# One transformer layer on one core: the last 256 tokens of the last down-product with tokens on partitions

## The chip, the cores and the metric

The kernel runs on one core of one Trainium2 chip. The metric is the device time of one execution in microseconds (us). The kernel before takes 1895.25 us, the median of three runs (1892.29 to 1896.35).

## The reference

One layer works on 1024 tokens of 1024 features, with 16 learned meta tokens ahead of them that are dropped at the end. All arithmetic is float32.

```
h = h + 0.5 * rmsnorm(swiglu(rmsnorm(h, g0), w_in[0], w_out[0]), g1)
h = h + rmsnorm(mlstm_mixer(rmsnorm(h, g2)), g3)
h = h + 0.5 * rmsnorm(swiglu(rmsnorm(h, g4), w_in[1], w_out[1]), g5)
return h[:, 16:]

swiglu(x)  = (silu(x @ w_in[:, :2816]) * (x @ w_in[:, 2816:])) @ w_out    # w_out: 2816 x 1024
rmsnorm(x) = x * rsqrt(mean(x * x) + 1e-6) * g                            # mean over the 1024 features
```

The change is in the last product by `w_out` (the "down product"), and in the norm, the addition of the residual h and the output that follow it.

## The kernel before

Features lie on the 128 partitions and tokens run along the free axis. A block of 512 tokens of the 1024 features is then 8 tiles of 128 x 512. A float32 product is done as three passes of matmuls in the format fp32r: each operand is split into a high and a low part, and high x high, high x low and low x high are summed in PSUM (`PASSES`). The split of a weight tile (`split_w`, lines 136 to 141) is a copy to fp32r on ScalarE (L139) and a subtraction on VectorE (L140).

Weights come by the DMA queue of SyncE (SPq) in the sequence of a list, `order`, into four raw buffers, are split in two halves into seven buffers, and are taken by `next_w`, which keeps loads and splits some tiles ahead. The 22 inner features (each 128 of the 2816) are cut into three segments, `SEGS`: 14 to 21, 0 to 7, and 8 to 13. The activations of one segment come back from DRAM by `load_a`, which splits them too (L327 on VectorE).

`down` does one segment for one block of tokens: for each of the 8 output tiles it takes a weight tile, runs the matmuls of its 6 or 8 inner features into a PSUM bank `pd` (L574, stationary = 128 x 128 of the weights, moving = the activations), and puts the sum into the result block `r`: ScalarE copies it for the first segment (L586), VectorE adds it for the others (L588). So each block has three sums per output tile.

The last down product has two blocks: C, the first 512 tokens, and E, the last 512. `downs` does C's three segments, then E's first two. The third segment of E is done twice, with its weights fetched a second time (names with `2x`): for E0 (E's first 256 tokens), then for E1 (the other 256). The norm of a block is a generator, `last_norm`: `rstd` squares the 8 result tiles (ScalarE), adds them on VectorE (L282), sums over partitions by a matmul with ones (`cb_ms`, L291), takes the root in 13 small steps on VectorE (L296 to L304), and brings the factors to all partitions by a matmul (`cb_rb`, L313) and a copy. Then two wide operations per tile follow, times gain and factor (L399) and plus residual (L400), and an output DMA. `tasks` and `tick` lay the steps of such generators between the matmuls of the product that runs beside them: C's norm lies in E's first segment, E0's norm in E1's third. E1's norm comes after all products, in a variant that divides the work among three engines (`fast`).

The program is written in this sequence; a scheduler of the framework then sets the sequence on each engine, and each engine works through its own in order.

Of the kernel before, what the change touches and what calls it, by code (L numbers as in the profile page):

```python
# [20 lines left out]
F32 = mybir.dt.float32  # L21
# [32 lines left out]
@with_exitstack  # L54
def trunk(ctx: ExitStack, tc: tile.TileContext, xa, xb, w1, w2, wqk, wv, wog, wo, par, cst, out):
    nc = tc.nc
# [326 lines left out]

    def last_norm(b, gi, scale, res, name, fast, queue=None):

        rs, n, e = R[b.i], b.n, b.s0 + b.n
        ret = []
        yield from rstd(lambda k: rs[:, k, b.s0 : e], n, scale, name, ret, fast)
        r = ret[0]
        for k in range(KT):  # L390
            y = rs[:, k, b.s0 : e]
            if fast:
                act.activation(y, y, AF.Copy, scale=gains[:, gi, k : k + 1])
        for k in (0, 1, 2, 3, 4, 7, 5, 6) if fast else range(KT):
            y = rs[:, k, b.s0 : e]
            if fast:
                (pool if k == 7 else vec).tensor_tensor(y, y, r[:, :n], ALU.mult)
            else:
                vec.scalar_tensor_tensor(y, y, gains[:, gi, k : k + 1], r[:, :n], ALU.mult, ALU.mult)  # L399
            (pool if fast and k in (0, 2, 7) else vec).tensor_tensor(y, y, res(k), ALU.add)  # L400
            if not fast:
                queue.dma_start(out[b.i, :, k, b.s0 : e], y)
            elif k in (1, 3, 5, 6):
                j = k - k % 2
                (act if k % 4 == 1 else sp).dma_start(
                    out[b.i, :, j : j + 2, b.s0 : e], rs[:, j : j + 2, b.s0 : e])
            yield

# [183 lines left out]

    def downs(li, b0, b1, Z, a0, second):
# [87 lines left out]
    tasks.append(split_x(A, 2, xh[0][0], range(4), "ca0"))  # L681
    c2 = next(phase)
    xh[0][1] = operand(Z[4], "xh0_1")
# [386 lines left out]
    es.close()  # L1070
    es_al, alp[0] = stage("al3", 4)

    def resid(k):
# [7 lines left out]
    res = block(Z[1], "res")  # L1081
    for k in range(0, KT, 2):
        pool.dma_start(res[:, k : k + 2, :512], h2[1][:, k : k + 2])
    c2 = next(phase)
    finish()
    E0, E1 = E.part(0, 256), E.part(256, 256)
    ends = [last_norm(q, 5, 0.5, lambda k, q=q: res[:, k, q.s0 : q.s0 + 256], f"cb1{q.s0}", q is E1, sp)
            for q in (E0, E1)]
# [4 lines left out]
    for _ in ends[1]:  # L1093
        pass
    es_al.close()


def _layout(inputs):
# [4 lines left out]
    def tiles(w):  # L1103
# [19 lines left out]
    return {  # L1123
        "xa": xt[:, :, :528], "xb": xt[:, :, 528:], "w1": w1, "w2": w2, "wqk": tiles(wa[:, 0:1024]), "wv": wv,
        "wog": tiles(wa[:, 2048:3072]), "wo": tiles(f["a_w_out"][0]), "par": par, "cst": cst,
# [16 lines left out]
```

## Time and profile before

| | us |
|---|---|
| median of the three runs | 1895.25 |
| profiled execution | 1892.53 |
| its span | 1890.4 |
| TensorE busy in it | 1854.1 (98%) |
| VectorE busy in it | 1283.0 (68%) |
| ScalarE busy in it | 750.2 (40%) |

The span runs from the first to the last instruction of one profiled execution; its own time is a little longer. The mean granted clock of TensorE was 0.994 of full speed. PE stands for matmuls on TensorE, PEld for its weight loads, DVE for VectorE, ACT for ScalarE, POOL for GpSimd, SP for SyncE. L574 is line 574 of the kernel before. A time such as 1620.24 is measured from the start of the span.

### The profile page before, as it was taken

How to read it: one execution, taken by the hardware profiler on the slowest of the kernel's cores; microseconds unless marked ns; L12 is line 12 of the kernel's file. 1: busy time of each engine (PE TensorE's matmuls, PEld its weight loads, DVE VectorE, ACT ScalarE, POOL GpSimd, SP SyncE). 2: the span in 40 equal slices, each digit the busy share in tenths (PEclk: the TensorE clock that was granted, in tenths of full speed). 3: DMA queues.
4: the chain of work that ended last, by engine and by line, in shares of the span. 5: the costliest groups of instructions: out<-in, count | busy, mean ns of one | idle time of the engine just before them, and what ended most of it. 6: DMA issues, size and time to landing. Idle time of an engine off the chain costs nothing.

```text
span 1890.4 us, 34012 instructions
## 1 busy us (share of the span) xinstructions
PE 1854.1 (98%) x13428; PEld 1733.9 (92%) x13428; DVE 1283.0 (68%) x2302; ACT 750.2 (40%) x1324; POOL 204.9 (11%) x367
## 2 busy tenths in 40 slices
PE   7999999999999999999999999999999999999995
PEld 7999999999999888999798878999999999888885
DVE  6857888887356746863774568686877777456547
ACT  5433332233334423544544445563332222344323
POOL 1210000000000002201002112221000000000100
PEclk9999999999999999999999999999999999999998
DMA  8655454445346424634435546765454444555633
GB/s 310 203 199 174 164 175 147 137 146 190 116 156 185 150 81 147 193 96 140 132 100 171 174 169 212 248 227 200 163 169 165 152 146 156 159 162 159 206 112 95
DMA packets 112270, 311.28 MB, mean 165 GB/s; under 512 B 14208, under 2 KB 24896, under 8 KB 112112
## 3 DMA queue, kind: packets, MB, share of 16 engines
q1 hardware_dynamic: 83280, 215.49, 36.5%
q0 software_dynamic: 28288, 93.10, 13.7%
q8 instruction: 106, 1.74, 0.4%
q10 hardware_dynamic: 544, 0.52, 0.1%
q14 instruction: 52, 0.43, 0.1%
HBM read 239.18 MB, written 69.88 MB: 163 GB/s over the span
## 4 chain that ended last, share of the span: by engine, by line
PE 92%; issue 3%; DMA 2%; DVE 2%; ACT 1%; POOL 0%; SPq 0%; DVEq 0%; POOLq 0%; ACTq 0%
PE pd L574 26%; PE py L417 13%; PE pw L417 13%; PE pz L417 7%; PE hy L417 6%; PE hx L417 6%; PE po L1003 5%; PE wog_ps L727 5%; PE wqk_ps L727 4%; PE pv L838 4%; PE pn L950 1%; DMA xa<-xa 1%; DMA o<-xa 1%; PE pn L944 0%; DMA W<-nmd 0%
## 5 line engine op out<-in xcount | busy, mean ns | idle before, releaser
L574 PE MATMUL pd<-a,w 128*128 128x512 f32 (+2 forms) x2640 | 481.1, 344 | 0.0
L574 PEld LDWEIGHTS pd<-a,w 128*128 128x128 f32 x2640 | 415.4, 188 | 62.9
L417 PE MATMUL py<-x,w1j_p 128*128 128x264 f32 (+1 forms) x2112 | 266.7, 282 | 0.0
L417 PE MATMUL pw<-x,w1j_p 128*128 128x264 f32 (+1 forms) x2112 | 266.7, 282 | 0.0
L417 PEld LDWEIGHTS pw<-x,w1j_p 128*128 128x128 f32 x2112 | 258.4, 188 | 0.0
L417 PEld LDWEIGHTS py<-x,w1j_p 128*128 128x128 f32 x2112 | 258.3, 188 | 0.0
L139 ACT CAST w1j_p<-w1j_s 128x512 fp32r<-128x512 f32 x176 | 109.3, 621 | 314.7 <-PE py L417 184.9
L140 DVE TENSOR_TENSOR w<-w_raw,w 128x512 fp32r<-128x512 f32 x192 | 123.4, 646 | 152.4 <-ACT w L139 152.1
L139 ACT CAST w<-w_raw 128x512 fp32r<-128x512 f32 x192 | 112.2, 585 | 209.6 <-PE pd L574 192.4
L417 PE MATMUL hx<-x,w1a 128*128 128x264 f32 (+1 forms) x1056 | 137.4, 286 | 10.4 <-ACT w1a L139 8.2
L417 PEld LDWEIGHTS hx<-x,w1a 128*128 128x128 f32 x1056 | 131.9, 191 | 11.1 <-ACT w1a L139 8.2
L417 PE MATMUL hy<-x,w1a 128*128 128x264 f32 (+1 forms) x1056 | 135.5, 283 | 2.7 <-DVE hc L446 2.4
L417 PE MATMUL pz<-x,w1j_p 128*128 128x264 f32 (+1 forms) x1056 | 133.4, 282 | 0.0
L417 PEld LDWEIGHTS hy<-x,w1a 128*128 128x128 f32 x1056 | 130.0, 189 | 3.5 <-DVE hc L446 2.8
L140 DVE TENSOR_TENSOR w1j_p<-w1j_s,w1j_p 128x512 fp32r<-128x512 f32 x176 | 121.8, 692 | 11.6 <-ACT w1j_p L139 9.9
L417 PEld LDWEIGHTS pz<-x,w1j_p 128*128 128x128 f32 x1056 | 129.2, 188 | 0.0
L838 PE MATMUL pv<-wv,xh 128*128 128x260 f32 (+1 forms) x864 | 108.3, 286 | 0.0
L838 PEld LDWEIGHTS pv<-wv,xh 128*128 128x128 f32 (+1 forms) x864 | 102.8, 179 | 3.8 <-issue 0.3
L727 PE MATMUL wqk_ps<-xh,wqk 128*128 128x264 f32 (+1 forms) x576 | 99.2, 327 | 0.0
L1003 PE MATMUL po<-xh,wo 128*128 128x512 f32 x384 | 96.2, 400 | 0.0
L727 PE MATMUL wog_ps<-xh,wog 128*128 128x264 f32 (+1 forms) x576 | 91.8, 321 | 0.0
L727 PEld LDWEIGHTS wog_ps<-xh,wog 128*128 128x128 f32 x576 | 82.6, 188 | 8.3
(350 smaller groups left out, 2246.7 us busy)
## 6 DMA issues: line engine op xcount, KB each, us to landing
w1j_raw<-w SPq DMA_DIRECT2D x88, 512.0 KB, 3.7
w_raw<-w SPq DMA_DIRECT2D x64, 512.0 KB, 3.7
w1a_raw<-w SPq DMA_DIRECT2D x43, 512.0 KB, 4.8
al<-a SPq DMA_DIRECT2D x66, 256.0 KB, 3.5
w_raw<-w SPq DMA_DIRECT2D x32, 384.0 KB, 3.2
a<-v POOLq DMA_DIRECT2D x44, 256.0 KB, 2.6
wv_raw<-wv SPq DMA_DIRECT2D x16, 520.0 KB, 3.5
h<-r POOLq DMA_DIRECT2D x16, 512.0 KB, 4.1
```

What stands on the lines that cost most here:

```text
L139: act.copy(t[:, 0, :n], src)
L140: vec.tensor_tensor(t[:, 1, :n], src, t[:, 0, :n].bitcast(F32), ALU.subtract)
L417: pe.matmul(ps[:, s * 512 : s * 512 + m], lhsT=w[:, wp_, k * P : (k + 1) * P], rhs=x[:, xp_, k, s * m : (s + 1) * m], start=(first and k = ...
L574: pe.matmul(ps[:, s * 512 : s * 512 + m], lhsT=w[i // 4][:, wp_, i % 4 * P : (i % 4 + 1) * P], rhs=a[i // 4][:, xp_, i % 4, b.s0 + s0 : b. ...
L727: pe.matmul(ps[:, s * 512 : s * 512 + m], lhsT=w[k // 4][:, wp_, k % 4 * P : (k % 4 + 1) * P], rhs=xh[h.i][k // 4][:, xp_, k % 4, s0 : s0 ...
L838: pe.matmul(ps[:L, :VW], lhsT=xh[h.i][k // 4][:, xp_, k % 4, t0 : t0 + L], rhs=w[k // 2][:, wp_, k % 2 * VW : (k % 2 + 1) * VW], start=(k ...
L950: pe.matmul(pn[e][:, j * 129 : (j + 1) * 129], lhsT=W[:, q], rhs=v[:, q, 0:129], start=False, stop=True, skip_group_check=True)
L1003: pe.matmul(ps[:, :512], lhsT=w[k // 4][:, wp_, k % 4 * P : (k % 4 + 1) * P], rhs=xh[h.i][k // 4][:, xp_, k % 4, 0:512], start=(k == 0 and ...
```

## The change

C is done as before. E0 now gets all three segments by itself, in products 256 wide, with the weights fetched once; its residual goes into the unused half of E's result block. C's norm pauses longer between its steps, takes each residual one step earlier, and its output leaves by GpSimd's queue. E1 is done last and the other way round: the stationary operand is 128 x 128 of the activations, so that the result has tokens on partitions, and the moving operand is 512 columns of `w_out` in its original layout (a new input, `w2t`). Two token tiles times two halves of the features are four PSUM banks, `pt`, which take all 22 inner features; so the third segment's activations of E1 are kept in a tile of their own (`cx`). The last three inner features are done bank by bank. E1's residual is transposed on TensorE (`residual_t`), the gain is loaded as a row on all partitions (`gr`). The norm of E1 then needs no sum over partitions: ScalarE squares a bank with a sum along its free axis, VectorE multiplies by the gain, the root is ScalarE's Sqrt with a reciprocal and one correcting step on VectorE. The output is one tensor, whose first 768 rows are put in order on the host.

```
-    def last_norm(b, gi, scale, res, name, fast, queue=None):
+    def last_norm(b, gi, scale, res, name, dst, pause=0):
...
+        h = res(0)
         for k in range(KT):
...
+            y, h0 = rs[:, k, :n], h
+            vec.scalar_tensor_tensor(y, y, gains[:, gi, k : k + 1], r[:, :n], ALU.mult, ALU.mult)
+            if k + 1 < KT:
+                h = res(k + 1)
+            for _ in range(1 + pause):
+                yield
+            vec.tensor_tensor(y, y, h0, ALU.add)
+            pool.dma_start(dst[:, k], y)
+            for _ in range(1 + pause):
+                yield
...
+        e = part or b1
...
-        down(b1, SEGS[0], c0, True)
+        down(e, SEGS[0], c0, True)
         yield
-        c2 = [operand(Z[6], f"a{li}_10"), operand(Z[0], f"a{li}_11")]
-        down(b1, SEGS[1], c1, False, load_a(b1, SEGS[2], c2))
-        yield c2
+        c2 = [operand(Z[6], f"a{li}_10"), operand(Z[0], f"a{li}_11") if part is None else rest]
+        down(e, SEGS[1], c1, False, load_a(b1, SEGS[2], c2))
+        yield c0, c1, c2
...
-    down_order(1, E, SEGS[2], "x")
+    order.extend(Plain(w2t[f], f"w2t_{f}") for fs in SEGS for f in fs)
...
+    gr = zp.tile([P, D], F32, name="gr")
+    pool.dma_start(gr, g5.to_broadcast([P, D]))
+    act.activation(gr, gr, AF.Copy, scale=0.5)
...
+    def residual_t(resT):
...
+                q[j] = tmp(f"rt{j}")
+                pool.dma_start(q[j][:, :512].rearrange("p (k t) -> p k t", k=2), h2[1][:, 2 * j : 2 * j + 2, 256:512])
...
+                        pe.transpose(ps[:, (2 * c + kk) * P : (2 * c + kk + 1) * P],
+                                     t[:, kk * 256 + c * P : kk * 256 + (c + 1) * P], ident)
+                act.copy(resT[:, :, (j - 1) * 256 : j * 256], ps.rearrange("p (c d) -> p c d", c=2))
...
-    phase = downs(1, C, E, Z, a0, (last_norm(C, 5, 0.5, resid, "cb0", False, pool), None))
+    phase = downs(1, C, E, Z, a0, (last_norm(C, 5, 0.5, resid, "cb0", outs[0], 2), None), E0, cx)
...
-    down(E0, SEGS[2], c2, False, None, ends[0])
-    tasks.append(ends[0])
-    down(E1, SEGS[2], c2, False, None, ends[1])
+    tasks.append(residual_t(resT))
+    end0 = last_norm(E0, 5, 0.5, lambda k: res[:, k], "cb1", outs[1])
+    down(E0, SEGS[2], c[2], False, None, end0)
+    tasks.append(end0)
...
+            pe.matmul(
+                pt[t][h],
+                lhsT=c[g][j // 4][:, xp_, j % 4, 256 + t * P : 256 + (t + 1) * P],
+                rhs=w[h][:, wp_, :512],
...
+    KEEP = 3
+    for i in range(NF - KEEP):
...
+        act.activation(q[:, :512], p, AF.Square, accum_out=ss[:, 2 * t + h : 2 * t + h + 1])
+        y = ready_y[t, h] = tmp(f"zy{t}{h}")
+        vec.tensor_tensor(y[:, :512], p, gr[:, h * 512 : (h + 1) * 512], ALU.mult)
...
+        act.activation(q, m, AF.Sqrt, bias=b, scale=1.0 / D)
+        vec.scalar_tensor_tensor(v, m, 1.0 / D, b, ALU.mult, ALU.add)
+        vec.reciprocal(r, q)
...
+            vec.scalar_tensor_tensor(y, y, r, resT[:, t, o], ALU.mult, ALU.add)
+            (act if t and h else sp).dma_start(outs[2][t, :, o], y)
```

On TensorE, in the first two output tiles of E's first segment before, C's factors are broadcast (`cb_rb`). In a name such as `w_1_1_14_3_512`, 14 is the segment's first inner feature and 3 the output tile:

```order
L574 MATMUL pd<-a_6_18355,w_1_1_14_0_0_18931 128x512 x12
L574 MATMUL pd<-a_7_18356,w_1_1_14_0_512_18934 128x512 x6
L291 MATMUL cb_ms<-ones,cb_acc 128x1 x4
L574 MATMUL pd<-a_7_18356,w_1_1_14_0_512_18934 128x512 x6
L574 MATMUL pd<-a_6_18355,w_1_1_14_1_0_18967 128x512 x12
L313 MATMUL cb_rb_19044<-ident,cb_y 128x128 x4
L574 MATMUL pd<-a_7_18356,w_1_1_14_1_512_18970 128x512 x12
```

On the same engine in the kernel after (its L568 is the line that was L574), from the start of E0:

```order
L568 MATMUL pd<-a_6_18362,w_1_1_14_0_0_18938 128x256 x12
L568 MATMUL pd<-a_7_18363,w_1_1_14_0_512_18941 128x256 x11
L291 MATMUL cb_ms<-ones,cb_acc 128x1 x4
L568 MATMUL pd<-a_7_18363,w_1_1_14_0_512_18941 128x256
L568 MATMUL pd<-a_6_18362,w_1_1_14_1_0_18974 128x256 x12
L568 MATMUL pd<-a_7_18363,w_1_1_14_1_512_18977 128x256 x12
L568 MATMUL pd<-a_6_18362,w_1_1_14_2_0_19029 128x256 x12
L568 MATMUL pd<-a_7_18363,w_1_1_14_2_512_19032 128x256 x12
L568 MATMUL pd<-a_6_18362,w_1_1_14_3_0_19075 128x256 x12
L568 MATMUL pd<-a_7_18363,w_1_1_14_3_512_19078 128x256 x3
L313 MATMUL cb_rb_19051<-ident,cb_y 128x128 x4
L568 MATMUL pd<-a_7_18363,w_1_1_14_3_512_19078 128x256 x9
```

The broadcast moved from the second output tile to the fourth, and the products between are half as wide.

On VectorE, the root of C's factors (L296 to L304) in the kernel after:

```order
L296 TENSOR_SCALAR cb_v<-cb_ms 128x4
L327 TENSOR_TENSOR a_10_19303<-al,a_10_19303 128x512
L297 TENSOR_SCALAR cb_y<-cb_v 128x4
L327 TENSOR_TENSOR a_10_19303<-al,a_10_19303 128x512
L298 TENSOR_SCALAR cb_y<-cb_y 128x4
L140 TENSOR_TENSOR w_1_1_14_4_0_19111<-w_1_1_14_4_raw,w_1_1_14_4_0_19111 128x512
L300 SCALAR_TENSOR_TENSOR cb_t<-cb_y 128x4
L140 TENSOR_TENSOR w_1_1_14_4_512_19114<-w_1_1_14_4_raw,w_1_1_14_4_512_19114 128x512
L301 TENSOR_TENSOR cb_t<-cb_t,cb_v 128x4
L327 TENSOR_TENSOR a_10_19303<-al,a_10_19303 128x512
L302 SCALAR_TENSOR_TENSOR cb_y<-cb_t,cb_y 128x4
L327 TENSOR_TENSOR cx<-al,cx 128x512
```

Before, one 128x512 operation stood between L296 and L297 and one between L301 and L302 of the third round; now ten stand among the 13 small ones, the first six of them in this piece.

On VectorE, the end of the kernel after, from the third bank's multiply by the gain (`pt_19896`, first half of the second token tile):

```order
L1152 TENSOR_TENSOR zy_20385<-pt_19896,gr 128x512
L1162 SCALAR_TENSOR_TENSOR ends<-ends 128x1
L1154 TENSOR_SCALAR ss<-ss 128x1
L1163 TENSOR_TENSOR ends<-ends 128x1
L1164 SCALAR_TENSOR_TENSOR ends<-ends 128x1
L1167 SCALAR_TENSOR_TENSOR zy_20357<-zy_20357,ends,resT 128x512
L1167 SCALAR_TENSOR_TENSOR zy_20362<-zy_20362,ends,resT 128x512
L1152 TENSOR_TENSOR zy_20399<-pt_19897,gr 128x512
L1160 SCALAR_TENSOR_TENSOR ends<-ss 128x1
L1161 RECIPROCAL ends<-ends 128x1
L1162 SCALAR_TENSOR_TENSOR ends<-ends 128x1
L1163 TENSOR_TENSOR ends<-ends 128x1
```

The first token tile's last two operations (L1167) stand ahead of the fourth bank's multiply; the second tile's root and its two L1167 follow.

## Rows read from the trace of the kernel before

**Rows 1.** The page: engines' busy time, chain by engine, a group of lines.
```profile
PE 1854.1 (98%) x13428; PEld 1733.9 (92%) x13428; DVE 1283.0 (68%) x2302; ACT 750.2 (40%) x1324; POOL 204.9 (11%) x367
...
PE 92%; issue 3%; DMA 2%; DVE 2%; ACT 1%; POOL 0%; SPq 0%; DVEq 0%; POOLq 0%; ACTq 0%
...
L139 ACT CAST w1j_p<-w1j_s 128x512 fp32r<-128x512 f32 x176 | 109.3, 621 | 314.7 <-PE py L417 184.9
```

**Rows 2.** Timeline, TensorE, last stage: start, length, operation, [idle before <- releaser].
```profile
1620.24 126.76 PE L574 MATMUL pd<-a,w 128*128 128x512 f32 x546
1746.84 0.95 PE L291 MATMUL cb_ms<-ones,cb_acc 128*128 128x1 f32 x8
...
1752.71 97.96 PE L574 MATMUL pd<-a,w 128*128 128x512 f32 x492
1850.51 2.27 PE L574 MATMUL pd<-a,w2x 128*128 128x256 f32 x18
...
1858.34 4.13 PE L574 MATMUL pd<-a,w2x 128*128 128x256 f32 x33
...
1864.31 6.62 PE L574 MATMUL pd<-a,w2x 128*128 128x256 f32 x54 [1.84 <-DVE r L588]
```

**Rows 3.** Timeline of all engines, from the last product to the end.
```profile
1870.97 0.42 DVE L588 TENSOR_TENSOR r<-r,pd 128x256 f32<-128x256 f32 x1 [0.79 <-PE pd L574]
...
1872.45 0.58 PE L291 MATMUL cb_ms<-ones,cb_acc 128*128 128x1 f32 x4 [1.51 <-DVE cb_acc L282]
...
1873.07 0.16 DVE L296 TENSOR_SCALAR cb_v<-cb_ms 128x2 f32<-128x2 f32 x1 [0.76 <-PE cb_ms L291]
1873.26 0.17 DVE L297 TENSOR_SCALAR cb_y<-cb_v 128x2 int32<-128x2 int32 x1
...
1875.74 1.20 PE L313 MATMUL cb_rb<-ident,cb_y 128*128 128x128 f32 x4 [2.72 <-DVE cb_y L304]
...
1877.38 2.15 DVE L397 TENSOR_TENSOR r<-r,cb_r 128x256 f32<-128x256 f32 x3 [1.78 <-ACT cb_r L321]
...
1882.86 0.74 DVE L400 TENSOR_TENSOR r<-r,res 128x256 f32<-128x256 f32 x2
```

**Rows 4.** Groups by line and shape, last stage: count | busy us, mean ns | idle before.
```profile
L588 DVE TENSOR_TENSOR r<-r,pd 128x512 f32<-128x512 f32 x24 | 16.5, 686 | 22.8 <-PE pd L574 22.8
...
L399 DVE SCALAR_TENSOR_TENSOR r<-r,pk,cb_r 128x512 f32<-128x512 f32 x8 | 5.6, 748 | 0.1
...
L279 ACT ACTIVATE cb_sq<-r 128x512 f32<-128x512 f32 x7 | 4.4, 633 | 0.3
```

**Rows 5.** Groups by line and shape, whole span, TensorE's transposes.
```profile
L989 PE MATMUL py<-ident,yt 128*128 128x128 f32 x64 | 9.6, 272 | 0.0
```

**Rows 6.** Timeline, VectorE, in C's norm.
```profile
1744.17 0.69 DVE L327 TENSOR_TENSOR a<-al,a 128x512 fp32r<-128x512 f32 x1
1744.77 0.69 DVE L282 TENSOR_TENSOR cb_acc<-cb_acc,cb_sq 128x512 f32<-128x512 f32 x1
...
1747.83 0.16 DVE L296 TENSOR_SCALAR cb_v<-cb_ms 128x4 f32<-128x4 f32 x1 [0.56 <-PE cb_ms L291]
1747.90 0.68 DVE L140 TENSOR_TENSOR w<-w_raw,w 128x512 fp32r<-128x512 f32 x1
```

**Rows 7.** Windows: from:to, length, busy PE PEld DVE ACT POOL, PEclk, DMA share, GB/s.
```profile
10.00:20.00 10.00, 7.46 (x39) 6.62 (x38) 5.90 (x9) 6.97 (x12) 0.42 (x1) 1.00 1.03 405
...
1750.00:1760.00 10.00, 10.00 (x48) 8.24 (x48) 8.39 (x17) 3.36 (x6) 2.16 (x4) 1.00 0.97 346
1760.00:1770.00 10.00, 10.00 (x45) 8.09 (x44) 6.92 (x12) 3.11 (x6) 2.17 (x4) 1.00 0.80 274
```

**Rows 8.** DMA issues, whole span, then 1740 to 1891: count, KB each, us to landing.
```profile
al<-a SPq DMA_DIRECT2D x66, 256.0 KB, 3.5
...
cb_h<-h SPq DMA_DIRECT2D x8, 256.0 KB, 5.1
...
out<-r SPq DMA_DIRECT2D x2, 256.0 KB, 2.4
```

More of the change, by code (lines that the diff above doesn't have):

```diff
@@ L54, in trunk @@
 @with_exitstack
-def trunk(ctx: ExitStack, tc: tile.TileContext, xa, xb, w1, w2, wqk, wv, wog, wo, par, cst, out):
+def trunk(ctx: ExitStack, tc: tile.TileContext, xa, xb, w1, w2, w2t, g5, wqk, wv, wog, wo, par, cst, out):
     nc = tc.nc
@@ L382, in split_x @@
             yield
-    def last_norm(b, gi, scale, res, name, fast, queue=None):
-        rs, n, e = R[b.i], b.n, b.s0 + b.n
+    def last_norm(b, gi, scale, res, name, dst, pause=0):
+        rs, n = R[b.i], b.n
         ret = []
-        yield from rstd(lambda k: rs[:, k, b.s0 : e], n, scale, name, ret, fast)
+        yield from rstd(lambda k: rs[:, k, :n], n, scale, name, ret)
         r = ret[0]
+        h = res(0)
         for k in range(KT):
[L391 to L407, printed above, removed]
+            y, h0 = rs[:, k, :n], h
[8 more added lines that the diff above has]
+                yield
     def shaped(t, n):
@@ L591, in down, with downs @@
                     next(g, None)
-    def downs(li, b0, b1, Z, a0, second):
+    def downs(li, b0, b1, Z, a0, second, part=None, rest=None):
+        e = part or b1
         a1 = [operand(Z[4], f"a{li}_2"), operand(Z[5], f"a{li}_3")]
@@ L1071, in trunk @@
     es_al, alp[0] = stage("al3", 4)
+    es_z, zp = stage("z")
+    E0 = E.part(0, 256)
+    outs = (
+        out[0:512].rearrange("(p a) (b t) -> p (a b) t", a=4, b=2),
+        out[512:768].rearrange("(p a) (b t) -> p (a b) t", a=2, b=4),
+        out[768:1024].rearrange("(c t) d -> c t d", c=2),
+    )
+    gr = zp.tile([P, D], F32, name="gr")
+    pool.dma_start(gr, g5.to_broadcast([P, D]))
+    act.activation(gr, gr, AF.Copy, scale=0.5)
     def resid(k):
@@ L1076, in resid @@
         return t[:, :512]
[L1078 removed]
+    cx = zp.tile([P, 2, 2, 528], F32R, name="cx")
+    def residual_t(resT):
+        q = {}
+        for j in range(5):
+            if j < 4:
+                q[j] = tmp(f"rt{j}")
+                pool.dma_start(q[j][:, :512].rearrange("p (k t) -> p k t", k=2), h2[1][:, 2 * j : 2 * j + 2, 256:512])
+                yield
+            if j:
+                t = q[j - 1]
+                ps = small.tile([P, 512], F32, name="prt", tag="ps")
+                for kk in range(2):
+                    for c in range(2):
+                        pe.transpose(ps[:, (2 * c + kk) * P : (2 * c + kk + 1) * P],
+                                     t[:, kk * 256 + c * P : kk * 256 + (c + 1) * P], ident)
+                act.copy(resT[:, :, (j - 1) * 256 : j * 256], ps.rearrange("p (c d) -> p c d", c=2))
+                yield
@@ L1079, in trunk @@
+    phase = downs(1, C, E, Z, a0, (last_norm(C, 5, 0.5, resid, "cb0", outs[0], 2), None), E0, cx)
     next(phase)
     next(phase)
-    res = block(Z[1], "res")
+    res = R[1][:, :, 264:520]
     for k in range(0, KT, 2):
-        pool.dma_start(res[:, k : k + 2, :512], h2[1][:, k : k + 2])
-    c2 = next(phase)
+        pool.dma_start(res[:, k : k + 2], h2[1][:, k : k + 2, 0:256])
+    c = next(phase)
     finish()
-    E0, E1 = E.part(0, 256), E.part(256, 256)
-    ends = [last_norm(q, 5, 0.5, lambda k, q=q: res[:, k, q.s0 : q.s0 + 256], f"cb1{q.s0}", q is E1, sp)
-            for q in (E0, E1)]
@@ L1089, in trunk @@
-    down(E0, SEGS[2], c2, False, None, ends[0])
-    tasks.append(ends[0])
-    down(E1, SEGS[2], c2, False, None, ends[1])
-    finish()
-    for _ in ends[1]:
-        pass
+    resT = slot(Z[2], "resT").bitcast(F32)[:, : 2 * D].rearrange("p (c d) -> p c d", c=2)
+    tasks.append(residual_t(resT))
+    end0 = last_norm(E0, 5, 0.5, lambda k: res[:, k], "cb1", outs[1])
+    down(E0, SEGS[2], c[2], False, None, end0)
+    tasks.append(end0)
+    pt = [bank("pt0"), [small.tile([P, 512], F32, name=f"pt1{h}", tag="ps") for h in range(2)]]
@@ new lines, in trunk, with step @@
+    pt = [[pt[0][:, 0:512], pt[0][:, 512:1024]], pt[1]]
+    ss = st.tile([P, 8], F32, name="ss", tag="ss")
+    small_ = st.tile([P, 16], F32, name="ends", tag="ends")
+    def step(i, w, t, h, ticks):
+        for pi, (wp_, xp_) in enumerate(PASSES):
+            g, j = (i // 8, i % 8) if i < 16 else (2, i - 16)
+            pe.matmul(
+                pt[t][h],
+                lhsT=c[g][j // 4][:, xp_, j % 4, 256 + t * P : 256 + (t + 1) * P],
+                rhs=w[h][:, wp_, :512],
+                start=(i == 0 and pi == 0),
+                stop=(i == NF - 1 and pi == 2),
+            )
+        if ticks:
+            tick()
@@ L1095, in trunk @@
+    for t in range(2):
+        for h in range(2):
+            for i, w in enumerate(ws):
+                step(NF - KEEP + i, w, t, h, False)
+            if t:
+                half_done(t, h)
+        if not t:
+            half_done(t, 0)
+            half_done(t, 1)
+        tile_done(t)
+    es_z.close()
     es_al.close()
```

33 lines of the change are left out of this document (29 added, 4 removed).

## The prediction

> **What bounds the kernel now.** I read the engines' shares and the chain of waits first [rows 1]. TensorE (PE in the rows) is busy for 98% of the span and carries 92% of the chain, so a change counts if it changes TensorE's work, lets it stand, or changes what follows its last product. Next came TensorE's timeline over the last stage [rows 2]. The reader is to see three things there: how long one matmul takes at each width, that TensorE stands only near the end, and where its last product ends. The width of 512 takes (1746.84 − 1620.24) / 546 = 0.2319 us. From 1752.71 to 1850.51 there are 348 of these and 144 of width 256, so a narrow one takes (97.80 − 80.70) / 144 = 0.1187 us. The last 87 products run from 1858.34 to 1870.93 (1864.31 + 6.62), 12.59 us, where 87 × 0.1187 = 10.33 would do: 2.26 us is stall, 1.84 of it one wait for VectorE. Third came the timeline of the tail [rows 3]. After 1870.93 nothing overlaps: sum of squares, the root in steps of 0.2 us (1873.07 to 1873.26), a broadcast, wide operations up to 1883.60 (1882.86 + 0.74), and then 6.80 us to the end of the span at 1890.40. The tail is 19.47 us.
>
> I write C for the first 512 tokens, E0 for the next 256, E1 for the last 256. C's last product ends at 1620.24 + 528 × 0.2319 = 1742.68; I call that T0, and up to there only one scaling of a gain row is added.
>
> **The change part by part.**
>
> *TensorE's products.* Before, after T0: 384 of width 512 and 288 of width 256, 89.05 + 34.19 = 123.24 us. After: all 22 inner features of E0 take 528 of width 256, 62.67 us; E1 takes 22 × 2 tiles × 2 halves × 3 passes = 264 of width 512, 61.22 us; together 123.89. That is +0.65. The matmuls of C's and E0's norms stand in both.
>
> *Transposes of E1's residual.* 16 new ones lie between E0's products. 64 of the same shape were busy 9.6 us [rows 5], 0.15 each, so +2.4. Lower bound 1.6 (0.1 each, if they pack like the products), upper 4.4 (0.272 each, the length of a record).
>
> *The old stall.* The VectorE wait at 1864.31 came because E1's sums shared VectorE with E0's norm. E1's sums now stay in four PSUM banks, so this goes: −2.26. What could be late there next is a split weight, and there is room for that (below).
>
> *The broadcast of C's factors.* This is the new wait. The order puts the broadcast in E0's fourth output tile. TensorE gets there at T0 + 0.8 (the sum-of-squares matmuls) + 3 × 24 × 0.1187 + 14 × 0.1187 = T0 + 11.0, twice as early as with 512 tokens. On VectorE the root's 13 small steps now stand among ten wide operations. They start when the sum of squares is there, at T0 + 3.5. A wide one takes 0.60 (1744.17 to 1744.77), a small one ahead of a wide one only 0.07 (1747.83 to 1747.90) [rows 6]; ten wide, ten hidden small, three at 0.2 give T0 + 10.8. So it is even, if the two loads of E's last activations in that stretch are in time. They leave at about T0 + 2.0 and T0 + 4.3 and are wanted at T0 + 5.4 and T0 + 8.1; the rows give 3.5 us to landing in general and 5.1 for such a load in the busy stretch [rows 8]. I take 0.7 us of standing, bounds 0 and 3. Behind the waiting matmul stands every later product.
>
> *VectorE in E0.* From T0 to its first addition into E0 it has 40 wide operations (32 at 0.60, 8 at 0.70) and 13 small, some 26 us; TensorE needs 9 × 2.85 + 1.6 = 27.3. That is full but in time: the splits of weights are queued two to three tiles ahead, by my count about 5 us before TensorE wants them at the tightest. The longer pauses of C's norm only put its last operations and its output further apart, and nothing of TensorE waits for those; after it the load falls to about 1.6 of 2.85 us per tile. Cost 0, and up to 1 us if an operand is late.
>
> *DMA in E0.* In the 31.3 us after T0 (eleven output tiles) the queues carry 9 weight tiles of 512 KB and 26 pieces of 256 KB (8 of C's residual, 8 of its output, 4 of E0's residual, 4 of E1's, 2 of activations): 11,264 KB, 11.53 MB. That asks for 368 GB/s. The rows show 405 and 346 GB/s with the queues full [rows 7]. At 346 it takes 33.3 us, 2 us late, inside the 5 us. Cost 0 in the sum. The Trainium skill, HBM Reference, Specifications, speaks against such a demand: it puts a core's share at about 358 GB/s when both cores of a domain stream, and about 425 for a core alone. By the share it would be about 1 us late, by the other figure in time; the 405 of this trace goes past the share. Neither changes the sum.
>
> *Weights of E1.* One inner feature is 12 × 0.2319 = 2.78 us of TensorE against two splits, 1.24 us on ScalarE and 1.38 on VectorE [rows 1, 6], and one load of 512 KB, 188 GB/s. All hidden. The gain row's load and scaling lie in the stage before T0, where ScalarE waits for TensorE anyway [rows 1]. On the SP queue C's residual stands between E0's weight loads, as before, now spread over more of them; E0's output moves from SP to POOL's queue, where nothing else is left. ScalarE's copies of the transposed residual go where C's sums were and wait until C's output has landed, about T0 + 34 by the DMA sum; their turn is at T0 + 51. The table load for the root stands between two of these copies, with casts queued two to three tiles ahead of TensorE. Cost 0.
>
> *The new tail.* E is TensorE's last product. The first token tile is complete 18 × 0.2319 = 4.17 us before E. Square 0.63, multiply 0.69, Square 0.63, multiply 0.69 [rows 4] follow each other, since in the program each multiply waits for the Square of its bank; with about 0.03 per hand-over that ends at E − 1.4. Then VectorE goes in order: two small, the third bank's multiply, four small, the first tile's two wide operations (0.70 each, 8 in 5.6 us [rows 4]), the fourth bank's multiply: 0.4 + 0.69 + 0.8 + 1.4 + 0.69 brings E + 2.6. The last bank's Square is done at E + 0.65, so its multiply is held over 1 us by the tile before. Then five small (1.0) and two wide (1.4): E + 5.0. The closing stays 6.80, since the last stores are 256 KB as before (2.4 us to landing [rows 8]). Tail 11.80, so −7.67. A Square with a sum is not in the trace; nearest is 0.63 without, upper bound twice that, which puts up to 1.3 us on the tail; nothing makes it shorter.
>
> *Sum.* TensorE's end: +0.65 + 2.4 + 0.7 − 2.26 = +1.49. Tail: −7.67. Together −6.2: the profiled execution's 1892.53 becomes 1886.3. That execution lies 2.7 below the median shown (1895.25); the mean of the three runs and this one is 1894.1, 1.6 above it. I put a new median there: 1887.9.
>
> **The rivals.**
>
> *1. The factors come late.* The two loads land 5 us or more after they leave, ScalarE's casts behind them slip, and the root ends 3 to 4 us after TensorE has come to the broadcast. For it: in the rows of this place VectorE stands for one 0.56 us only [rows 6], and the margin is 0.2 us. Against it: the loads have 3.4 and 3.8 us, about what the general median needs. Price 3 to 4 us over my 0.7, so 1891 to 1892.
>
> *2. The queues can't feed E0.* Slower than before. Between T0 and T0 + 31.3 weights, residual and output want 11.53 MB. Past 5 us of lateness TensorE stands for weights. That begins under 11.53 / 36.3 = 318 GB/s, and the whole gain of 6.2 is gone under 11.53 / 42.5 = 271. The second window of C's norm gave 274 GB/s [rows 7], though with the engines 80% busy, so it was asked for no more. At 250 GB/s it takes 46.1 us, 9.8 past the slack, and the time is 1897.7. Against it: 346 at 97% just before.
>
> *3. The end is longer than worked out.* Squares with a sum at their upper bound and transposes at 0.272: 1.3 + 2.0 = 3.3 more, so 1891.2.
>
> **How the numbers follow.** Forecast 0.70, first rival 0.13, second 0.08, third 0.09. A measurement tells about 0.2% from no change, 3.8 us. The forecast's own bounds run from −8 to −4 around medians that spread by 2 us: 1884 to 1891. The first and third fall at the edge of no change, the second is slower. So faster 0.71, same 0.20, slower 0.09, and a range from 1883.5 to 1893, which leaves out the second rival and the worst of the first.
>
> **What would show it.** In the changed profile: TensorE's last product about 1.5 us later than 1870.93; no wait of TensorE at the end of E0; a wait of under 1 us, or none, at the broadcast of C's factors; E1's products without a gap at 0.232 us; the last wide operation 5.0 us after the last product, with the fourth bank's multiply held behind the first tile's; and 6.8 us of closing. I am wrong if TensorE waits more than 3 us in E0, if E0's products wait for ScalarE or DMA, or if the closing grows.

## The result

The changed kernel takes 1882.34 us (median of four runs, 1881.48 to 1883.97) against 1895.80 for the kernel before in the same comparison: ratio 0.9931, interval 0.9919 to 0.9943. A second comparison (e8 below) gave 1884.81 against 1893.66: 0.9948, 0.9935 to 0.9962. It is faster, and by more than was forecast. The profiled execution took 1881.98 us, its span 1880.2.

The page of the kernel after, engines' busy time and chain by engine, hardly differs from [rows 1]:

```profile
PE 1853.1 (99%) x13556; PEld 1738.7 (92%) x13556; DVE 1294.1 (69%) x2310; ACT 768.3 (41%) x1352; POOL 209.8 (11%) x376
...
PE 91%; issue 4%; DMA 2%; DVE 1%; ACT 1%; POOL 1%; DVEq 0%; POOLq 0%; ACTq 0%
```

TensorE's timeline of the kernel after (start, length, operation, [idle before <- releaser]) answers to [rows 2]. L313 is the broadcast, L1100 the transposes, L1126 the products of E1:

```profile
1619.82 125.30 PE L568 MATMUL pd<-a,w 128*128 128x512 f32 x551
...
1746.01 7.86 PE L568 MATMUL pd<-a,w 128*128 128x256 f32 x64
1755.64 1.16 PE L313 MATMUL cb_rb<-ident,cb_y 128*128 128x128 f32 x8 [1.77 <-DVE cb_y L304]
1756.55 36.67 PE L568 MATMUL pd<-a,w 128*128 128x256 f32 x309
...
1793.77 0.60 PE L1100 MATMUL prt<-ident,rt 128*128 128x128 f32 x4
...
1799.01 0.95 PE L568 MATMUL pd<-cx,w 128*128 128x256 f32 x6
...
1819.59 45.46 PE L1126 MATMUL pt<-w2t,a 128*128 128x512 f32 x195
1864.89 1.55 PE L1126 MATMUL pt<-w2t,cx 128*128 128x512 f32 x6
...
1871.15 1.55 PE L1126 MATMUL pt<-w2t,cx 128*128 128x512 f32 x6
```

The reader is to see one wait, 1.77 us, at the broadcast; no other in E0; E1's products at (1864.89 − 1819.59) / 195 = 0.2323 us each; and the last product's end at 1872.70, against 1870.93 before. Between 1793.77 and 1799.01 lie the four groups of transposes and 30 narrow products: 5.24 − 30 × 0.1187 = 1.7 us for the 16 transposes.

The timeline of the tail of the kernel after answers to [rows 3]. L1150 is the Square, L1152 the multiply by the gain, L1167 the two last wide operations of a token tile, L1168 the stores:

```profile
1868.57 0.60 ACT L1150 ACTIVATE zq<-pt 128x512 f32<-128x512 f32 x1 [4.25 <-PE pt L1126]
...
1872.73 0.60 ACT L1150 ACTIVATE zq<-pt 128x512 f32<-128x512 f32 x1 [1.13 <-PE pt L1126]
1872.82 1.41 DVE L1167 SCALAR_TENSOR_TENSOR zy<-zy,ends,resT 128x512 f32<-128x512 f32 x2
1873.23 0.19 ACT L1150 ACTIVATION_READ_ACCUMULATOR zq<-pt 128x1 f32 x1
...
1874.15 0.68 DVE L1152 TENSOR_TENSOR zy<-pt,gr 128x512 f32<-128x512 f32 x1
...
1875.59 1.41 DVE L1167 SCALAR_TENSOR_TENSOR zy<-zy,ends,resT 128x512 f32<-128x512 f32 x2
1877.03 0.38 ACTq L1168 DMA_DIRECT2D out<-zy  x1
```

VectorE's last operation ends at 1877.00, 4.3 us behind the last product. The last bank's Square is done at 1873.42, and its multiply starts at 1874.15, held 0.73 us by the first tile's L1167: the order that was worked out, where the hold was put at over 1 us. From 1877.00 to the end of the span are 3.2 us; before it was 6.8.

Where the time went is read best from the start of the last down product, since the unchanged part ahead of it began that product anywhere between 1619.7 and 1623.9 us in the profiles of this study, of either kernel. All in us, from the timelines:

| | start | to the last product's end | from there to VectorE's last operation | from there to the end | sum |
|---|---|---|---|---|---|
| before | 1620.24 | 250.70 | 12.67 | 6.82 | 270.19 |
| after | 1619.82 | 252.88 | 4.31 | 3.20 | 260.39 |
| forecast | | +1.5 | −7.7 | 0 | −6.2 |
| measured | | +2.18 | −8.36 | −3.62 | −9.80 |

The closing, the last column but one, is what the forecast lacked.

The waits of SyncE's queue in the last 20 us (waited for: us in total, times, longest) show it. Of the kernel before:

```profile
SPq L1137 <- PEq L1137: 3.9, 2, 3.4
SPq L1137 <- DMA out<-r: 1.8, 2, 1.1
```

Of the kernel after:

```profile
SPq L1224 <- DMA out<-zy: 2.1, 2, 1.4
SPq L1224 <- PEq L1224: 0.6, 2, 0.5
```

Before, SyncE had seen its stores land and then stood 3.4 us at the meeting of all engines that ends the program. The view names PE's sequencer, but such a wait is for all engines; the instructions of that line show who came last. GpSimd's and SyncE's drains of the kernel before (count: shortest/median/longest ns, first and last start):

```profile
L1137 POOLq DRAIN  x3: 40/93/10075, 1879.6 to 1890.2; - x3
L1137 SPq DRAIN  x3: 7/7/7, 1886.4 to 1889.9; - x3
```

The same of the kernel after:

```profile
L1224 POOLq DRAIN  x3: 40/93/4488, 1830.7 to 1879.9; - x3
L1224 SPq DRAIN  x3: 7/7/7, 1879.4 to 1879.7; - x3
```

SyncE was ready at 1886.4, but GpSimd's drain, begun at 1879.6 beside its last additions, took 10.08 us and ended at 1889.65. After, GpSimd has nothing to do in the tail, its drain is over at 1835.2, and the program ends about 1 us behind the last store.

### The profile page after: what moved, and what is told of

Its sections match the earlier page's. It is cut to its first block, busy times and chain, and to the rows that moved or that the text cites. A ratio compares the mean times of both kernels' runs of the same rounds, so it can differ in the third digit from the quotient of the medians.

```text
span 1880.2 us, 34386 instructions
## 1 busy us (share of the span) xinstructions
PE 1853.1 (99%) x13556; PEld 1738.7 (92%) x13556; DVE 1294.1 (69%) x2310; ACT 768.3 (41%) x1352; POOL 209.8 (11%) x376
## 4 chain that ended last, share of the span: by engine, by line
PE 91%; issue 4%; DMA 2%; DVE 1%; ACT 1%; POOL 1%; DVEq 0%; POOLq 0%; ACTq 0%
PE pd L568 23%; PE py L411 13%; PE pw L411 13%; PE pz L411 7%; PE hy L411 6%; PE hx L411 6%; PE po L999 5%; PE wog_ps L723 5%; PE wqk_ps L723 4%; PE pv L834 4%; PE pt L1126 3%; PE pn L946 1%; DMA o<-xa 1%; DMA W<-nmd 1%; PE pn L940 0%
## 5 line engine op out<-in xcount | busy, mean ns | idle before, releaser
L568 PE MATMUL pd<-a,w 128*128 128x264 f32 (+2 forms) x2592 | 433.2, 328 | 0.0
L568 PEld LDWEIGHTS pd<-a,w 128*128 128x128 f32 x2592 | 383.7, 188 | 46.1
```

What stands on the lines that cost most here:

```text
L568: pe.matmul(ps[:, s * 512 : s * 512 + m], lhsT=w[i // 4][:, wp_, i % 4 * P : (i % 4 + 1) * P], rhs=a[i // 4][:, xp_, i % 4, b.s0 + s0 : b. ...
```

## The experiments

Edits are against the kernel named; "sum" is the last column of the table above, and "closing" the column before it. e5, e6, e7 and e10 to e18 were run and profiled once each, so their numbers are those of one trace. In the traces with the changed kernel's own tail (after, e3, e4, e8) the part from the last product to VectorE's last operation agrees within 0.01 us and the closing within 0.02; the part ahead of them does not, since the wait at the broadcast varies (see e3).

**e1: the kernel before, its tail without GpSimd.**

```
-                (pool if k == 7 else vec).tensor_tensor(y, y, r[:, :n], ALU.mult)
+                vec.tensor_tensor(y, y, r[:, :n], ALU.mult)
-            (pool if fast and k in (0, 2, 7) else vec).tensor_tensor(y, y, res(k), ALU.add)
+            vec.tensor_tensor(y, y, res(k), ALU.add)
```

> The kernel before, with the four wide operations of GpSimd in the last norm done by VectorE. Theory (GpSimd's closing drain): in the trace before, GpSimd's last operation ends at 1880.98 and its drain at 1889.65, 8.67 us later, while the last store has landed at 1886.4; the closing of 6.80 us is the drain's. Then the closing falls to about 3.4 us, the tail's VectorE work grows by 4 x 0.335 = 1.3 us, and the time falls by about 2 us. Rival (the closing belongs to the last stores and the end of the program): the closing stays 6.8 us and the time grows by 1.3 us.

Measured: 1890.10 against 1894.50, ratio 0.9976 (0.9967 to 0.9985); sum 266.14, 4.05 less than before. The closing is 3.59, so 3.2 of it was GpSimd's. The drain is still there, 12.05 us long, but it begins at 1792.4, beside the last transfers that GpSimd issues, and is over long before the tail:

```profile
L1137 POOLq DRAIN  x3: 40/93/12050, 1792.4 to 1887.6; - x3
```

The rest was not expected: the wide operations did not take 1.3 us more but 0.78 less (11.89 in the table's third column). VectorE's timeline in e1:

```profile
1878.79 0.76 DVE L397 TENSOR_TENSOR r<-r,cb_r 128x256 f32<-128x256 f32 x2 [1.78 <-ACT cb_r L321]
1879.46 0.75 DVE L400 TENSOR_TENSOR r<-r,res 128x256 f32<-128x256 f32 x2
...
1883.49 0.75 DVE L400 TENSOR_TENSOR r<-r,res 128x256 f32<-128x256 f32 x2
```

Every pair starts 0.67 behind the one before it. In [rows 3] three L397 beside GpSimd stretch to 2.15 us, and the timeline of the kernel before goes on:

```profile
1879.46 0.94 DVE L400 TENSOR_TENSOR r<-r,res 128x256 f32<-128x256 f32 x1
...
1880.32 1.27 DVE L397 TENSOR_TENSOR r<-r,cb_r 128x256 f32<-128x256 f32 x2
```

So three took 2.08 us from start to start (1879.46 − 1877.38), where three alone take 1.0, and the fourth 0.86; the four that stretch start 0.87 apart in the mean. Four operations of GpSimd took 1.34 us off VectorE and cost it 2.1. The Trainium skill, GPSIMD Engine Reference, Specifications, says that GpSimd shares its SBUF interfaces with VectorE, with contention when VectorE has two SBUF inputs, as here. The trace agrees, with 0.87 us from start to start in place of 0.335.

**e2 and e5: one, and four, additions on GpSimd in the changed kernel's tail.** In e5 the last line stands four times, on shifted columns.

```
+        if not t:
+            gp = tmp("gp")
+            pool.tensor_tensor(gp[:, :256], ready_y[0, 1][:, :256], resT[:, 0, :256], ALU.add)
```

> The changed kernel, with one addition of 128x256 on GpSimd, whose result nobody uses, once the first token tile of E1 is done (about 1873.5). Theory (drain): GpSimd ends it at about 1874.5, drains for 8.7 us to 1883.2, and the span ends 0.75 us behind that, at 1883.9 in place of 1880.2: 3.7 us slower. Rival (the closing belongs to the stores): no change, since the last store lands at 1879.1 as before.

> The changed kernel with four additions of 128x256 on GpSimd, one behind the other, in the place of the one in e2; nobody uses their result. In e2 GpSimd's drain ended only 1.57 us after its one operation, in the kernel before 8.68 us after the last of four. Theory A (the drain grows with the operations that GpSimd has been given): the four end at about 1879.5, the drain about 8 us later, and the span is some 5 to 6 us longer than in e2. Theory B (the long drain came of VectorE and GpSimd working on the same blocks with both operands in SBUF): the drain ends about 1.6 us after the last of the four, ahead of the last store, and the span is e2's, up to 1 us longer if VectorE's last two wide operations run beside GpSimd's at 0.945 us or more.

Measured: e2 sum 259.99, e5 260.92, closing 3.2 in both (e2 took 1884.25 us, e5 1882.35 in one run). The theory that a drain takes 8.7 us behind any operation fell: it ended 1.57 us behind the last one in e2 and in e5, before the stores. Theory A fell too. In e5 VectorE's last operation came 1.35 us later than in the changed kernel, beside GpSimd's additions, and that is in its sum. The drain in e2:

```profile
L1227 POOLq DRAIN  x3: 40/102/2318, 1876.4 to 1882.6; - x3
```

**e6: the kernel before with one GpSimd operation**, against e1:

```
-            vec.tensor_tensor(y, y, res(k), ALU.add)
+            (pool if fast and k == 0 else vec).tensor_tensor(y, y, res(k), ALU.add)
```

> The kernel before with only one operation of the tail on GpSimd (the first addition of the residual); the other three go to VectorE. Theory A (drain grows with the number of operations): the drain ends 1.6 us after the operation, hidden by the stores; the closing from VectorE's last operation to the end is 3.6 us as in e1, and VectorE loses one operation of 0.335 us and gains about 0.6 us beside GpSimd. Theory B (same blocks, both operands in SBUF): the drain is again several us long, and the closing is longer than 3.6 us if the drain passes the last store.

Measured: sum 267.89, closing 5.03; theory A fell, and theory B came out. GpSimd's operation, and its drain:

```profile
1879.20 0.83 POOL L400 TENSOR_TENSOR r<-r,res 128x256 f32<-128x256 f32 x1 [85.28 <-DVE r L397]
```

```profile
L1137 POOLq DRAIN  x3: 40/102/9547, 1879.2 to 1889.2; - x3
```

The drain ends at 1888.71, 8.67 us behind the one operation, as behind the last of four before. One operation is enough to make the closing long.

**e10, e11, e12: the last transfers of GpSimd's queue.** e10 is e6 with E's residual loaded by SyncE after E's second segment, e11 is e6 with it in eight loads, e12 is e2 with four more loads:

```
e10, behind the second segment:
-        pool.dma_start(res[:, k : k + 2, :512], h2[1][:, k : k + 2])
+        sp.dma_start(res[:, k : k + 2, :512], h2[1][:, k : k + 2])
e11:
-    for k in range(0, KT, 2):
-        pool.dma_start(res[:, k : k + 2, :512], h2[1][:, k : k + 2])
+    for k in range(KT):
+        pool.dma_start(res[:, k, :512], h2[1][:, k])
e12:
+    for k in range(0, KT, 2):
+        pool.dma_start(R[1][:, k : k + 2, :512], h2[1][:, k : k + 2])
```

> e6 (the kernel before with one GpSimd operation in the tail), with E's residual loaded by SyncE's queue instead of GpSimd's, one segment later. In e6 GpSimd's drain ended 8.68 us after its operation, in the changed kernel with the same operation (e2, e5) 1.57 us; the number of operations does not decide it. Theory C (the drain clears up behind the last transfers that GpSimd's own queue has issued: four loads of 512 KB in the kernel before, eight stores of 128 KB in the changed one): here the queue's last transfers are eight stores of 256 KB, and the drain ends 1.5 to 4 us after the operation; the closing from VectorE's last operation to the end falls from 5.0 to 3.6 us. Rival (the length belongs to the operation or to the place in this kernel): 8.7 us and 5.0 us as in e6.

> e6 with E's residual still on GpSimd's queue, but in eight loads of 256 KB instead of four of 512 KB; the last four transfers of the queue then hold half the bytes. Theory C with the size of one transfer as what counts: the drain ends about half as late, 4 to 5 us after the operation, and the closing is 3.6 us. Theory C with the bytes or the number of pieces in all: 8.7 us and 5.0 us, as in e6.

> e2 (the changed kernel with one GpSimd operation at the end), with four loads of 512 KB, which nobody reads, as the last transfers of GpSimd's queue, some 40 us before the end. Theory C: the drain ends about 8.7 us after the operation instead of 1.57, past the last store, and the span from the start of the last down product grows from 260.0 to about 263.5 us. Rival (the length belongs to the kernel before's operation or place): 1.57 us and 260.0 us, as in e2.

Measured behind the operation: e10 8.35, e11 9.00, e12 1.90 us. Theory C fell: in e10 and e12 in every form, in e11 in the form that goes by the size of one transfer (by the bytes in all, 8.7 was expected there). But each transfer more or less moved the drain by some 0.08 us.

**e13 and e14: VectorE's work beside the drain.** e13 is e1 with the last tile's addition on GpSimd; e14 is e2 with eight additions of 128x256 on VectorE behind GpSimd's.

```
e13:
-            vec.tensor_tensor(y, y, res(k), ALU.add)
+            (pool if fast and k == 6 else vec).tensor_tensor(y, y, res(k), ALU.add)
e14:
+            gv = tmp("gv")
+            for j in range(8):
+                vec.tensor_tensor(gv[:, :256], ready_y[0, 0][:, :256], resT[:, 0, :256], ALU.add)
```

> The kernel before with only the very last operation of the tail (the addition of the residual in the last tile) on GpSimd. In e6, e10 and e11, one operation on GpSimd early in the tail, VectorE goes on with ten or more additions and products of two SBUF operands, and the drain ends 8.3 to 9.0 us after GpSimd's operation; the queue's last transfers do not decide it (e10 to e12). Theory D (the drain is held while VectorE runs such operations): here VectorE has none left, the drain ends about 1.6 us after GpSimd's operation, ahead of the last store, and from GpSimd's last operation to the end are about 3.6 us. Rival (the drain takes 8.5 us behind any operation in this kernel): the drain ends 8.5 us after it and the end is 9.3 us behind it.

> e2 (the changed kernel with one GpSimd operation once the first token tile is done), with eight additions of 128x256 of two SBUF operands on VectorE behind it, whose result nobody uses. Theory D: GpSimd's drain, 1.57 us behind its operation in e2, now ends several us behind it. Rival: it ends 1.57 us behind it as in e2. Either way VectorE's own chain grows by 8 x 0.335 = 2.7 us, and the end by that.

Measured: e13 8.67, with nothing left on VectorE, and a closing of 10.04 (sum 272.29, longer than before); e14 1.57. Theory D fell.

**e15 and e16: place and use.** e15 puts the addition of e2 behind VectorE's last operation; e16 is e1 with an addition into a tile that nobody reads.

```
e15:
+    gp = tmp("gp")
+    pool.tensor_tensor(gp[:, :256], ready_y[1, 1][:, :256], resT[:, 1, :256], ALU.add)
e16:
+            if fast and k == 0:
+                gp = tmp("gp")
+                pool.tensor_tensor(gp[:, :256], y, res(k), ALU.add)
```

> The changed kernel with one addition of 128x256 on GpSimd behind VectorE's last operation, whose result nobody uses; in e2 the same operation stood 3.3 us earlier, with TensorE's last products just done. Theory F (what counts is the place: so far every long drain began when TensorE had been idle for over 3 us, every short one sooner): the drain ends 8.3 to 9 us behind the operation and the end is about 6 us later than without it, 266 us from the start of the last down product. Rival (what counts is the kernel's operands): the drain ends 1.6 to 1.9 us behind it and the end is as in the changed kernel, 260 us.

> e1 (the kernel before without GpSimd in the tail), with one addition of 128x256 on GpSimd once the first tile is done, written to a tile of its own that nobody reads, as in e2. Theory F (place: TensorE idle for over 3 us): the drain ends 8.3 to 9 us behind it and the closing is about 5 us, as in e6. Rival (what counts is that GpSimd wrote a part of the result block that a store then reads): the drain ends 1.6 to 1.9 us behind it and the closing is 3.6 us.

Measured: e15 1.57, e16 8.67. Theory F fell.

**e17 and e18: late transfers.** e17 is e6 with the stores of `ends` on GpSimd's queue; e18 is e2 with E0's on SyncE's, for which `last_norm` is given a queue.

```
e17:
-    ends = [last_norm(q, 5, 0.5, lambda k, q=q: ..., f"cb1{q.s0}", q is E1, sp)
+    ends = [last_norm(q, 5, 0.5, lambda k, q=q: ..., f"cb1{q.s0}", q is E1, pool)
e18:
-    end0 = last_norm(E0, 5, 0.5, lambda k: res[:, k], "cb1", outs[1])
+    end0 = last_norm(E0, 5, 0.5, lambda k: res[:, k], "cb1", outs[1], 0, sp)
```

> e6 (the kernel before with one GpSimd operation in the tail), with E0's eight stores of 128 KB on GpSimd's queue instead of SyncE's, so that the queue's last transfers, some 15 us ahead of the tail, are those of the changed kernel. Theory G (GpSimd's drain is long when its queue has issued nothing for 75 us or more ahead of it, and short behind transfers up to 45 us old): the drain ends 1.5 to 2.5 us behind the operation and the closing falls from 5.0 to 3.6 us. Rival: 8.3 to 9.0 us and 5.0 us as in e6.

> e2 (the changed kernel with one GpSimd operation at the end), with E0's eight stores on SyncE's queue, so that GpSimd's last transfer is some 90 us ahead of the end. Theory G: the drain ends 8.3 to 9 us behind the operation, past the last store, and the span from the start of the last down product grows from 260.0 to about 263.5 us. Rival: 1.57 us and 260 us as in e2.

Measured: e17 1.00, below the 1.5 to 2.5 expected, and a closing of 3.47, as expected; e18 0.91, where 8.3 to 9 was expected. So how old the last transfer is does not decide it, and theory G fell. Theory B fell with e17, where the operations are e6's on the same blocks. The drains of e17 and of e18:

```profile
L1137 POOLq DRAIN  x3: 40/102/1872, 1881.3 to 1889.5; - x3
```

```profile
L1227 POOLq DRAIN  x3: 40/102/1660, 1876.4 to 1882.5; - x3
```

What orders all of them is the number of transfers that GpSimd's queue has issued in the whole program (counted in the view of DMA issues):

| transfers | 348 | 352 | 356 | 357 | 360 | 365 | 369 |
|---|---|---|---|---|---|---|---|
| drain behind the operation, us | 8.35 | 8.67 | 9.00 | 0.91 | 1.00 | 1.57 | 1.90 |
| runs | e10 | before, e6, e13, e16 | e11 | e18 | e17 | e2, e5, e14, e15 | e12 |

It rises by 0.081 us per transfer from 348 to 356 and by 0.083 from 357 to 369, and falls by 8.1 between 356 and 357. Bytes do not order them: e6 and e11 move the same 93.10 MB by this queue. Two things weaken the count. 356 and 357 are runs of two different kernels; in the kernel before by itself the fall lies between 356 and 360 (e17), and in the changed kernel by itself none is seen. And e17 lies 0.16 us under the line through e18, e2 and e12. It looks like a list of transfers that is worked off at the end, and that was emptied once in between. That reading was formed from these runs and not tried on one of its own; why it falls there is open.

**e3 and e4: the wait at the broadcast.** e3 issues E0's residual loads behind E0's second segment; e4 puts 12 more steps between root and broadcast in `rstd` for C.

```
e3, the line moved from behind the loads of E0's residual to ahead of them:
+    c = next(phase)
e4:
-        for _ in range(1 if fast else 3):
+        for _ in range((1 if fast else 3) + late):
```

> The changed kernel, with the loads of E0's residual (1 MB on GpSimd's queue) issued after E0's second segment instead of at E0's start. Theory (DMA traffic at E0's start makes the two loads of E's last activations land in 6.1 us, so the root is late and TensorE waits 1.77 us at the broadcast of C's factors): the loads land in about 4 us, the wait falls below 0.5 us, and the time falls by 1.3 to 1.8 us. Rival (the loads are late because of what stands ahead of them on their own queue): they land as late as now, the wait stays 1.8 us and the time does not change.

> The changed kernel, with the broadcast of C's factors 21 products (2.5 us) later on TensorE; VectorE's order in the root is as it was. Theory (the wait of 1.77 us at the broadcast is lost time of TensorE): the wait goes and the time falls by 1.8 us. Rival (TensorE would wait somewhere else in E0 for what is queued behind, splits or loads): the wait shows up at a product of E0 and the time falls by less than 0.5 us.

Measured: e3 1883.53 us, wait 0.88, sum 259.40; e4 1883.51 us, no wait there, sum 259.17. Neither is told from the changed kernel by its time. e3 settles nothing: with the order as in the changed kernel, the wait differed from profile to profile just as much. In nine profiles it goes with the landing of the two loads of E's last activations (median of the two, from issue):

| | e14 | e7 | e12 | e18 | e5 | e15 | e8 | e2 | after |
|---|---|---|---|---|---|---|---|---|---|
| loads' landing, us | 4.6 | 4.7 | 4.8 | 4.9 | 5.3 | 5.4 | 5.6 | 5.7 | 6.1 |
| wait at the broadcast, us | 0.3 | 0.5 | 0.6 | 0.7 | 1.0 | 1.1 | 1.4 | 1.4 | 1.8 |

e3, with 5.2 and 0.9, lies on the same line. In the trace of the kernel after, the way from the load to the wait can be followed: ScalarE stands for the first of the two loads, VectorE for ScalarE's cast of it, in the middle of the root, and TensorE for the end of the root.

```profile
1750.90 0.62 ACT L326 CAST cx<-al 128x512 fp32r<-128x512 f32 x1 [2.41 <-DMA al<-a]
```

```profile
1751.56 0.69 DVE L327 TENSOR_TENSOR cx<-al,cx 128x512 fp32r<-128x512 f32 x1 [1.59 <-ACT cx L326]
```

In e4 TensorE's timeline has the broadcast without a wait, and one in E0 further on:

```profile
1757.76 1.05 PE L313 MATMUL cb_rb<-ident,cb_y 128*128 128x128 f32 x8
1758.57 18.68 PE L568 MATMUL pd<-a,w 128*128 128x256 f32 x156
1777.64 2.59 PE L568 MATMUL pd<-a,w 128*128 128x256 f32 x20 [0.39 <-DVE r L582]
```

To the last product e4 took 251.68, and e14, whose wait was 0.3, 251.35: part of the 1.77 came back as a wait for VectorE's additions, as the rival said, though 1.20 of it stayed gone and the rival had put that at under 0.5.

**e7: separate banks for the first token tile.**

```
-    pt = [bank("pt0"), [small.tile([P, 512], F32, name=f"pt1{h}", tag="ps") for h in range(2)]]
-    pt = [[pt[0][:, 0:512], pt[0][:, 512:1024]], pt[1]]
+    pt = [[bank(f"pt0{h}")[:, 0:512] for h in range(2)],
+          [small.tile([P, 512], F32, name=f"pt1{h}", tag="ps") for h in range(2)]]
```

and `half_done(t, h)` behind each bank of either tile.

> The changed kernel, with the two banks of the first token tile as two tiles, so that the first half's Square and multiply start when that half is complete (2.1 us earlier) instead of when both halves are. Theory (VectorE is the chain behind the last product, with the first tile's two wide operations on it): these run before the last product ends, and the last wide operation ends 3.6 us after the last product instead of 4.3; the span from the start of the last down product is 0.7 us shorter (259.7 in place of 260.4). Rival (the last bank's own Square, multiply, root and two operations are the chain already): no change.

Measured: 3.62 from the last product to VectorE's last operation instead of 4.31, as expected; sum 258.61, of which 1.2 of the gain is its shorter wait at the broadcast. E1's products took 0.28 longer (62.56 in place of 62.28), nearly all of it at two products behind VectorE's reading of E0's last sum (it ends at 1811.83, and the first of the two starts at 1811.98). That they wait for the bank of that sum is likely, but was not tried. VectorE's timeline in e7 shows the first tile's L1167 ahead of the last product's end (1873.17):

```profile
1871.21 1.41 DVE L1167 SCALAR_TENSOR_TENSOR zy<-zy,ends,resT 128x512 f32<-128x512 f32 x2
...
1873.93 0.69 DVE L1152 TENSOR_TENSOR zy<-pt,gr 128x512 f32<-128x512 f32 x1 [0.64 <-ACT zq L1150]
...
1875.37 1.41 DVE L1167 SCALAR_TENSOR_TENSOR zy<-zy,ends,resT 128x512 f32<-128x512 f32 x2
```

**e8 and e9: the changed kernel again, and e3, e4 and e7 together.**

> The changed kernel itself, again, on the same chip and in the same rounds as e9: the level that e9 is compared with. Expected: 0.69% below the kernel before, as at first, and 260.4 us from the start of the last down product to the end of the span (the part ahead of it has varied by 3 us from one profile to another).

> The changed kernel with e3, e4 and e7 together: residual loads later, broadcast of C's factors 21 products later, separate banks for the first token tile. If each gives its share (the wait of 1.77 us, the 0.7 us behind the last product): 2 to 2.5 us shorter from the start of the last down product to the end, 258 in place of 260.4, and 0.10 to 0.13% below e8. Rival (the wait moves into E0's products, as 0.39 us of it did in e4): 1 to 1.5 us.

Measured: e8 1884.81 us (1883.38 to 1885.34), sum 259.88; e9 1883.33 (1882.39 to 1884.67), sum 258.85. e9 is the lower by 1.5 us, 0.08%, and by 1.0 in the sum, the rival's size; the runs overlap, so this is not told from no change. Its ratio to the kernel before is 0.9943 (0.9931 to 0.9956).

## Why the prediction was wrong

Direction and mechanism were right: tokens on partitions spare the sum over partitions, the broadcast and the long tail. The size was too small, and one step made nearly all of the difference: "The closing stays 6.80, since the last stores are 256 KB as before". Only some 3.6 us of the 6.80 were the stores' and the program's end. GpSimd worked in the old tail, and its drain, 8.67 us behind its last addition, ended 3.3 us after SyncE had seen its stores land. The change took GpSimd out of the tail, and the closing fell to 3.20. The forecast looked at [rows 8], where 2.4 us to landing leave 4.4 of the 6.80 without a row, and did not ask who came last at the end of the program. e1 shows the cause alone: without GpSimd's four operations the old kernel's closing is 3.59. In the changed kernel a second thing would have done the same: the drain takes 1.57 us there, so that even with GpSimd in the tail the closing is 3.2 (e2). e1 shows also that 4.05 of the 9.80 us were to be had from the old tail without any new layout.

The two columns ahead of the closing were off by +0.7 and −0.7 us, which cancel; that is luck. The first time is partly luck too: the medians fell by 13.5 us in the first comparison and by 8.9 in the second, while the profiles put 9.8 us on the changed part. The rest, up or down, is the size of the spread ahead of that part.

The other steps, in their order:

- Products, +0.65: they ran at the rates of [rows 2], with E1's at 0.2323 us.
- Transposes, 2.4 with bounds 1.6 and 4.4: 1.7 us, near the lower bound; they pack like the products.
- The old stall, −2.26: gone, no wait at the end of E0.
- The broadcast, 0.7 with bounds 0 and 3: 1.77 in this profile, 0.3 to 1.8 in nine with this order. The place and the loads named were right; the landing of 3.5 to 5.1 [rows 8] was 4.6 to 6.1. In this profile the two loads landed over 5 us after they left, which was the first rival's condition, but its 3 to 4 us more did not come: the wait was 1.1 us over the 0.7, as the view gives it. Why they land late is open.
- These four make +1.86; measured were +2.18. Most of the other 0.3 lies at the same wait: from the first of the 64 products ahead of the broadcast to the broadcast are 9.63 us, where 64 × 0.1187 = 7.60 would do. Taken as the old stall was, the wait cost 2.03 us and not 1.77.
- VectorE and the queues in E0, 0: TensorE waited there only at the broadcast. In these windows of the kernel after (columns as in [rows 7]) the queues are full and TensorE is busy throughout, so the second rival did not come:

```profile
1764.00:1774.00 10.00, 10.00 (x87) 10.00 (x87) 10.00 (x17) 5.34 (x10) 3.66 (x6) 1.00 0.98 333
1774.00:1784.00 10.00, 10.00 (x88) 10.00 (x87) 6.97 (x13) 4.42 (x8) 1.98 (x3) 1.00 0.97 346
```

- The new tail, 5.0 to VectorE's last operation: 4.31, in the order worked out. The durations were taken a little long: the wide operations start 0.60 to 0.67 apart, not 0.70. The Square with a sum takes 0.60 and 0.19 for its sum, 0.69 in all and not twice 0.63, so the third rival did not come either.
- The median was put 1.6 us above the profiled execution. It lay 0.4 above it at first; e8's median was 2.5 us higher than the first. In the profiled executions the part ahead of the change spreads by more than that.

## What to carry to other kernels

The end of a program is a stage of its own: look up which engine comes last at the final meeting before putting the closing down to the last store, and if it is GpSimd, price its work in the tail with its drain. An engine that helps another over the same path to memory may cost it more than it takes off. A term that hangs on the landing of a load in busy queues is given as a range, not as the median of the whole program.

## What the runs showed of the hardware that was not expected

GpSimd's closing drain took from 0.91 to 9.00 us behind its last operation, by 0.08 us per transfer that its queue had issued, with a fall of 8.1 us between 356 (e11, the kernel before) and 357 (e18, the changed one). Beside GpSimd's operations on SBUF, VectorE's 128x256 operations on two SBUF operands took 0.87 us from start to start instead of 0.335, and in e5 some of its 128x1 operations took up to 0.69 instead of 0.15.
